# Delta-rule stage: the order on TensorE prices changes between plain and rounded matmuls and holds fill matmuls together in fours

## The chip, the cores and the metric

The kernel runs on one core of one Trainium2 chip. The metric is the device time of one execution in microseconds (us), the median over several runs. The core has TensorE (PE in the profile, with its weight loads as PEld), VectorE (DVE), ScalarE (ACT), GpSimd (POOL) and DMA queues issued from SyncE (SP).

## The reference

One layer of a hybrid backbone over 1024 latent tokens of width 1024, with 256 context tokens in front. The parts that matter here:

- `h = rms_norm(x) * (1 + scale) + shift`, then one input projection `h @ w_in` into many column groups: q, k, v of branch A, its gate z, q, k, v and gate of branch B, and merge gates.
- Branch A, the gated delta rule, in chunks of 128 tokens here (8 heads, two directions, 2 context chunks and 8 latent chunks each). Per chunk the state goes on as
  `v_new = u - w @ S`, `S' = S * exp(g_last) + k_dec^T @ v_new`, and the output is `q_dec @ S + qk @ v_new`. The triangular inverse behind `u` and `w` is made ahead of this, once for each head.
- Branch B, differential softmax attention (8 heads, two score maps each).
- Both branches are gated, projected, merged and sent through the output projection.

All results are float32.

## The kernel before, in words

The program is one long order of instructions per engine, written by a planner in Python when the kernel is built. Every piece of work is a generator ("stream") that yields steps of the form (engine, planned duration, what it depends on, how to issue it). The planner keeps a clock for each engine, asks each stream for its next step, chooses one, issues it and moves that engine's clock on. What it decides is only the order in which instructions stand on the engines; the chip then runs each engine's list in that order, and waits at semaphores where data is not there. There are two choosers. `flow` (line 75) takes, of all streams, the step with the smallest planned start plus bias. `turn_flow` (line 100) picks among steps that could start first on the same engine, within 0.02 us, by a priority; for the attention these come from the table `ABIAS` (line 1746), to which `due` (line 1438) adds 1.0 per tile of scores.

The stages in order of time are: the front (modulation, norm, transposes) and the convolution of q, k, v, both by `turn_flow`; the delta rule with everything that runs beside it, by `flow` (line 786); the attention and the merge of branch A, again by `turn_flow`; the output of branch B and the last projection.

In the stage that `flow` orders, TensorE has two kinds of work:

- **Fill.** The projections that nothing here waits for. Each operand is held as a rounded high part and a rounded low part (type fp32r), and a product is three rounded matmuls (high by high, high by low, low by high). `part_flow` (line 929) makes q, k, v of branch B in ten parts with outputs 256 wide, and then `fill_flow` (line 905) makes 32 gate units of 128 columns, each unit two halves of 24 matmuls 512 wide. In the profile their tile is `mm`. The fill stream has no bias (`None`): it takes part in the choice with its planned start plus `FB0`, and so stands back by 0.05 us for any other step. `FB1` would take over from `FT` = 38 finished units on, but there are only 32.
- **Plain float32 matmuls** of the delta rule. `scan` (line 1289) is the recurrence, one stream for each direction. A chunk is three dependent matmuls with a VectorE or ScalarE step between each two: `chain<-S,sk`, then `r` on VectorE, `chain<-r,x`, then `vd` on ScalarE, `chain<-vd,kk`, then `S` on VectorE. `out_chunk` adds two matmuls `out`. A plain matmul of 128 columns is two rows in the profile. `gdn_prep` (line 1082) prepares a head: `gram` matmuls in five groups, a substitution of 31 steps on VectorE, then four bursts of small matmuls (`pz`, `p`, `pz`, `pu`), and a store. Two preps are under way at a time: that of head h starts when head h-2 is stored, and `gram`, the substitution and the bursts each go head by head. The scan of a head needs the stored prep of that head and the scan of the head before.

For a step that needs a VectorE or ScalarE result, the planner reckons with a hand-over of 0.26 or 0.27 us plus `PEL` = 0.35 us before a matmul may be planned (table `LATENCY`, line 40).

`weights` and `part_weights` load and split the fill's weights into high and low parts on ACT, DVE and POOL; their bias is `WB` (line 1480). `flow` ends when the last head's tail (`tails`, line 1362: norm, gate, transposes `oT`) is planned and at least 32 - `LEFT` = 29 gate units are done. The rest of the gate units run in the next stage while the attention starts: its scores (`s`), softmax, transposes (`t`) and values (`v`) need memory that the delta rule gives free. In the attention, `sums`, `outs`, `lows` and `scales` are the queues of sums of squares, of squares of the outputs, of the low parts of transposed weights, and of the scaling of the second score map on ACT or POOL.

Of the kernel before, what the change touches and what calls it, by code (L numbers as in the profile page):

```python
# [34 lines left out]
PE, DVE, ACT, POOL, DMA, ADMA, DV2, PL1 = range(8)  # L35
# [8 lines left out]
class Block:  # L44
# [30 lines left out]
    def flow(self, until):  # L75


        clk = self.clk
        while not until():
            best = None  # L80
            for s in self.streams:
                self.ask(s)
            for s in self.streams:
                self.ask(s)
                h = s[2]
                if h is None or callable(h):
                    continue
                if s[3] is None:
                    s[3] = self.ready_at(h[0], h[2])
                start = self.begin_at(h[0], s[3])  # L90
                if s[1] is None:
                    start += self.FB0 if self.units_done < self.FT else self.FB1
                if h[0] == PE and len(h) > 4 and self.heat - self.HEAT * (start - clk[PE]) < 0:
                    start += self.COLD
                if best is None or start + (s[1] or 0.0) < best[0]:
                    best = (start + (s[1] or 0.0), s)
            assert best, "no stream can go on"
            self.step(best[1])

    def turn_flow(self, until):  # L100
# [613 lines left out]
    def run(self):  # L714
# [4 lines left out]
        with ExitStack() as left:  # L719
            self.hp, self.hs = self.spool(left, "hp"), {}  # L720
            self.hgroup(0)
            with ExitStack() as lw, ExitStack() as cx:
# [21 lines left out]
                with tc.manual_schedule(engines={E.PE, E.DVE, E.Activation, E.Pool, E.SP}):  # L744
# [25 lines left out]
                    def more():  # L770
                        yield lambda: sum(self.posted) == sum((NL if k == "q" else NT) // 2 for k, _ in parts)
                        cx.close()
                        self.gdn_more(gr)
                        yield lambda: False
                    for g, b in ((self.scan(0), "scan"), (self.scan(1), "scan"), (self.forever(self.outq[0]), "outq"),
# [4 lines left out]
                        self.stream(g, self.BIAS[b]) if g is not first else self.streams.append([g, self.BIAS[b], head, None])  # L780
                    self.stream(self.part_weights(parts), self.WB)
                    self.stream(self.weights(todo), self.WB)
                    self.stream(more())
                    self.stream(fill(), None)
                    self.MW = 2.5
                    self.flow(lambda: self.tailed == H and self.units_done >= len(todo) - self.LEFT)
                    gr.close()
# [645 lines left out]
    def named(self, n, gen):  # L1433
        s = self.entry[n] = [gen, self.ABIAS.get(n, 0), None, None]
        s[2] = next(gen, None)
        self.streams.append(s)

    def due(self, n, i):

        self.entry[n][1] = self.ABIAS.get(n, 0) + self.DUE * i  # L1440

# [35 lines left out]
    SPI = 0.5  # L1477
    MW = 0.0
    LAND = 2.5
    WB = -0.17  # L1480
    FT = 38
    LEFT = 3
    FB0 = 0.05
    FB1 = 0.36
    COLD = 0.4
    HEAT = 0.55
    HMAX = 0.55
# [244 lines left out]
    def side_start(self):  # L1732
# [10 lines left out]
    ONACT = (1, 2, 3)  # L1743
    TOL = 0.02
    PACE = 4.48
    ABIAS = dict(rels=-0.59, softs=8.84, norms=5.82, gateq=-27.29, sums=-18.71,
                 outs=-21.73, lows=-2.4, highs=-9.33, adds=36.19, scales=31.0, evs=22.29, mouts=-3.31,
                 att_out=1.9, turns=3.19, scores=-21.22, merge=25.46)
    KEEP = 3

# [454 lines left out]
```

## Time and profile before

| what | us |
|---|---|
| median of 3 runs (lowest to highest) | 1943.65 (1940.72 to 1945.57) |
| the profiled execution, its own time | 1943.38 |
| its span, first to last instruction | 1941.5 |
| PE busy in the span | 1901.2 |
| DVE busy | 1451.9 |
| ACT busy | 1065.9 |
| POOL busy | 679.2 |

A row of the profile is an instruction or a group of equal ones: start, length, engine, line, what it writes and reads, shape and count. All matmuls have the same line, that of a helper, and are told apart by their tiles. The ends of matmul rows are modelled and rows overlap, so what a matmul costs is read from start to start, not from the length of its row.

### The profile page before, as it was taken

How to read it: one execution, taken by the hardware profiler on the slowest of the kernel's cores; microseconds unless marked ns; L12 is line 12 of the kernel's file. 1: busy time of each engine (PE TensorE's matmuls, PEld its weight loads, DVE VectorE, ACT ScalarE, POOL GpSimd, SP SyncE). 2: the span in 40 equal slices, each digit the busy share in tenths (PEclk: the TensorE clock that was granted, in tenths of full speed). 3: DMA queues.
4: the chain of work that ended last, by engine and by line, in shares of the span. 5: the costliest groups of instructions: out<-in, count | busy, mean ns of one | idle time of the engine just before them, and what ended most of it. 6: DMA issues, size and time to landing. Idle time of an engine off the chain costs nothing.

```text
span 1941.5 us, 37467 instructions
## 1 busy us (share of the span) xinstructions
PE 1901.2 (98%) x13807; PEld 1675.8 (86%) x13807; DVE 1451.9 (75%) x3613; ACT 1065.9 (55%) x2191; POOL 679.2 (35%) x610
## 2 busy tenths in 40 slices
PE   6999999999999999999999999999999999999999
PEld 4888888899999998888888878887898888888887
DVE  4687998948886888767864965337896979985577
ACT  4543444426233563677575645448885868883222
POOL 3200000005541332343433232325766657671203
PEclk9999999999999999999999999999999999999999
DMA  9144535575546557667686565665436474226542
GB/s 333 61 133 99 138 95 132 130 197 174 171 134 190 167 187 230 231 197 241 197 284 206 186 189 164 215 237 185 143 114 207 160 241 152 82 88 218 187 148 87
DMA packets 383038, 336.39 MB, mean 173 GB/s; under 512 B 142609, under 2 KB 323443, under 8 KB 381831
## 3 DMA queue, kind: packets, MB, share of 16 engines
q1 hardware_dynamic: 382855, 333.99, 54.6%
q8 instruction: 109, 1.79, 0.4%
q14 instruction: 74, 0.61, 0.1%
HBM read 222.14 MB, written 111.79 MB: 172 GB/s over the span
## 4 chain that ended last, share of the span: by engine, by line
PE 83%; DVE 6%; DMA 4%; ACT 3%; issue 2%; SPq 1%; POOL 1%; DVEq 0%; ACTq 0%; POOLq 0%
PE mm L56 42%; PE s L56 6%; PE v L56 5%; PE chain L56 5%; PE mb L56 5%; PE ma L56 4%; PE x L56 3%; PE t L63 3%; PE out L56 3%; DVE S L1562 1%; PE gram L56 1%; DVE ac L595 1%; PE tr L63 1%; PE pz L56 1%; PE mp L56 1%
## 5 line engine op out<-in xcount | busy, mean ns | idle before, releaser
L56 PE MATMUL mm<-hs,wh 128*128 128x512 f32 (+1 forms) x2048 | 648.3, 390 | 1.5 <-DVE hs L408 1.4
L56 PEld LDWEIGHTS mm<-hs,wh 128*128 128x128 f32 x2048 | 371.1, 189 | 58.6 <-DVE hs L408 1.9
L56 PE MATMUL mm<-hs,wl 128*128 128x512 f32 (+1 forms) x1024 | 397.4, 388 | 1.0 <-POOL wl L885 1.0
L56 PE MATMUL mm<-wh,hs 128*128 128x256 f32 (+1 forms) x1792 | 332.7, 286 | 0.2 <-ACT sq L977 0.2
L56 PEld LDWEIGHTS mm<-wh,hs 128*128 128x128 f32 x1792 | 280.8, 191 | 0.7 <-ACT sq L977 0.4
L1562 DVE TENSOR_SCALAR_CACHE_REDUCE S<-s,rsq 128x512 f32<-128x512 f32 (+1 forms) x384 | 239.0, 654 | 27.6 <-PE s L56 14.2
L56 PE MATMUL mm<-wl,hs 128*128 128x256 f32 (+1 forms) x896 | 255.6, 285 | 0.0
L1599 POOL TENSOR_TENSOR S<-S 128x1280 f32<-128x1280 f32 x64 | 188.6, 2951 | 90.6 <-ACT S L1592 88.5
L56 PEld LDWEIGHTS mm<-hs,wl 128*128 128x128 f32 x1024 | 193.8, 189 | 29.8 <-POOL wl L885 1.4
L1575 ACT ACTIVATE S<-S,mn 128x1280 f32<-128x1280 f32 x128 | 175.2, 1371 | 53.2 <-DVE mn L1574 53.1
L56 PEld LDWEIGHTS mm<-wl,hs 128*128 128x128 f32 x896 | 171.3, 191 | 0.1
L595 DVE SCALAR_TENSOR_TENSOR ac<-xc,convT,ac 128x1284 f32<-128x1284 f32 (+1 forms) x96 | 138.8, 1448 | 11.5 <-ACT ac L593 10.8
L56 PE MATMUL s<-kk,qh 128*128 128x512 f32 (+1 forms) x384 | 143.6, 374 | 2.3 <-DVE S L1562 1.7
L56 PE MATMUL s<-kk,ql 128*128 128x512 f32 (+1 forms) x384 | 133.8, 360 | 0.0
L1636 DVE TENSOR_TENSOR al<-t,ah 128x512 fp32r<-128x512 f32 (+1 forms) x192 | 106.8, 595 | 7.6 <-ACT ah L1631 6.2
L580 POOL MEMSET xc<- 128x2 f32 (+1 forms) x64 | 3.6, 99 | 298.2 <-ACT sq L629 113.2
L1157 DVE TENSOR_TENSOR ts<-ts,tmp 80x31 f32<-80x31 f32 (+15 forms) x248 | 93.8, 378 | 6.0
L1155 DVE TENSOR_TENSOR tmp<-ab,ts 80x31 f32<-80x31 f32 (+15 forms) x248 | 91.4, 368 | 6.1 <-DMA ab<-da 0.7
L56 PE MATMUL ma<-y,wh 128*128 128x512 f32 x256 | 93.3, 410 | 1.9 <-DVE g L1808 1.9
L1320 ACT ACTIVATE vd<-chain,edk 128x128 f32<-128x128 f32 x144 | 52.2, 370 | 75.8 <-PE chain L56 70.4
L1631 ACT CAST ah<-t 128x512 fp32r<-128x512 f32 (+1 forms) x192 | 87.8, 520 | 9.3 <-PE t L63 8.9
L56 PE MATMUL v<-al,vh 128*128 128x256 f32 x320 | 90.7, 284 | 0.4 <-DVE al L1636 0.3
(296 smaller groups left out, 4317.1 us busy)
## 6 DMA issues: line engine op xcount, KB each, us to landing
wr<-in_w_in_dram SPq DMA_DIRECT2D x48, 512.0 KB, 5.7
hx<-in_w_in_dram SPq DMA_DIRECT2D x64, 256.0 KB, 4.2
x<-xq SPq DMA_DIRECT2D x64, 256.0 KB, 5.0
X<-gcd SPq DMA_DIRECT2D x8, 1280.0 KB, 8.8
kd<-col SPq DMA_DIRECT2D x40, 256.0 KB, 2.2
xq<-X SPq DMA_DIRECT2D x16, 640.0 KB, 8.8
kk<-kd SPq DMA_DIRECT2D x16, 640.0 KB, 5.8
kq<-gkq SPq DMA_DIRECT2D x8, 1152.0 KB
```

Source lines behind the costliest of these rows:

```text
L56: self.nc.tensor.matmul(out, lhsT, rhs, start=start, stop=stop)
L63: self.nc.tensor.transpose(out, src, self.ident[:src.shape[0], :src.shape[0]])
L580: x["e"].append((yield PL1, 0.1, [old], lambda: nc.gpsimd.memset(xc[:, a:b], 0.0)))
L595: t = yield DV2, 1.21e-3 * wd, [t], lambda: nc.vector.scalar_tensor_tensor(ac[:, :wd], xc[:, j:j + wd], self.convw(j, x["ct"]), ac[:, :wd] ...
L1155: t = yield DV2, n * w / 960.0 + 0.08, [t if j else self.later(t, 2.5), t1], lambda: V.tensor_tensor(tv, ab[:, j + 1:, j:j + 1].to_broadca ...
L1157: t = yield DV2, n * w / 960.0 + 0.08, [t, t1], lambda: V.tensor_tensor(ts[:, j + 1:, :w], ts[:, j + 1:, :w], tv, ALU.subtract)
L1320: td = yield ACT, 0.251, [t], lambda: nc.scalar.activation(vd, pc[:, 1], AF.Copy, scale=self.edk[:, c, g:g + 1])
L1562: e = yield DVE, 0.675 if m == 512 else 0.408, [e, self.sfree[c].get(n - 4 + c)], lambda: self.nc.vector.tensor_scalar(x["S"][c][:, o:o + ...
L1575: x["x"].append((yield ACT, 1.36, [e], lambda: nc.scalar.activation(S, S, AF.Exp, bias=x["mn"][:, c:c + 1], scale=-1.0, accum_out=w["l0"][ ...
L1599: e = yield POOL, 2.9, [e], lambda: self.nc.gpsimd.tensor_tensor(S0, S0, S1, ALU.add)
L1631: e = yield ACT, 0.48 if nb == 4 else 0.27, [t, y["old", k]], lambda: self.nc.scalar.copy(y["ah", k][:, :, q], pv)
L1636: t = yield DVE, 0.603 if k < 2 else 0.322, [e, y["old", k]], lambda: self.nc.vector.tensor_tensor(y["al", k][:, :, q], pv, y["ah", k][:, ...
```

## The change

In `flow` only, four things are new.

1. `SWITCH`: a fill step that follows a step of another stream on TensorE gets 0.086 us added to its planned duration.
2. `SWF`: right after such another step, the fill stands back by a further 0.2 us, 0.25 us with `FB0`.
3. `RUN`, `SWC`: after one, two or three fill matmuls in a row, a step of any other stream on TensorE stands back by 0.62 us. From the fourth on it doesn't.
4. `streak` counts this: the number of fill matmuls in a row, or -1 after another step.

Then weights are different: `WB` goes from -0.17 to -0.38 (the weight streams take part in the choice 0.21 us earlier), `FB1` from 0.36 to 0.46, and in the attention's table `sums` and `outs` come later (by 2.82 and 7.78), `lows` and `scales` sooner (by 2.11 and 3.7). No instruction is added or removed; what moves is the order on the engines and the DMA queue.

```diff
@@ flow
                 if s[1] is None:
                     start += self.FB0 if self.units_done < self.FT else self.FB1
+                    start += self.SWF if self.streak < 0 else 0.0
+                elif h[0] == PE and 0 < self.streak < self.RUN:
+                    start += self.SWC
...
             assert best, "no stream can go on"
+            if best[1][2][0] == PE:
+                fill = best[1][1] is None
+                if fill and self.streak < 0:
+                    h = best[1][2]
+                    best[1][2] = (h[0], h[1] + self.SWITCH) + tuple(h[2:])
+                self.streak = max(self.streak, 0) + 1 if fill else -1
             self.step(best[1])
@@ class Block
-    WB = -0.17
+    WB = -0.38
     FT = 38
     LEFT = 3
+    SWITCH, RUN, streak = 0.086, 4, 0
+    SWF = 0.2
+    SWC = 0.62
     FB0 = 0.05
-    FB1 = 0.36
+    FB1 = 0.46
...
-    ABIAS = dict(rels=-0.59, softs=8.84, norms=5.82, gateq=-27.29, sums=-18.71,
-                 outs=-21.73, lows=-2.4, highs=-9.33, adds=36.19, scales=31.0, evs=22.29, mouts=-3.31,
+    ABIAS = dict(rels=-0.59, softs=8.84, norms=5.82, gateq=-27.29, sums=-15.89,
+                 outs=-13.95, lows=-4.51, highs=-9.33, adds=36.19, scales=27.3, evs=22.29, mouts=-3.31,
                  att_out=1.9, turns=3.19, scores=-21.22, merge=25.46)
```

## The prediction

> **What bounds the kernel now.** I read the page's totals and its chain first, then the busy time in stretches cut at the stage borders, then what TensorE waited for, and last the order of matmuls inside the delta rule.
>
> ```profile
> PE 83%; DVE 6%; DMA 4%; ACT 3%; issue 2%; SPq 1%; POOL 1%; DVEq 0%; ACTq 0%; POOLq 0%
> ```
>
> ```profile
> 752.00:1269.00 517.00, 513.32 (x4588) 448.57 (x4587) 341.18 (x1006) 317.22 (x930) 180.10 (x238) 1.00 0.68 215
> ...
> 1320.00:1330.00 10.00, 5.94 (x31) 4.33 (x30) 4.88 (x17) 9.47 (x13) 4.16 (x2) 1.00 0.44 147
> 1330.00:1340.00 10.00, 10.00 (x65) 9.27 (x64) 7.24 (x25) 6.62 (x12) 4.85 (x2) 0.83 1.03 379
> 1340.00:1720.00 380.00, 375.54 (x2444) 331.84 (x2442) 326.27 (x1106) 299.74 (x506) 255.22 (x128) 1.00 0.46 154
> ```
>
> The columns of a stretch are its length, busy time of PE, PEld, DVE, ACT and POOL with instruction counts, granted clock, DMA share and GB/s. TensorE carries 83% of the chain and is covered by rows nearly everywhere: 513.3 of 517 us while the scans run. The one visible hole is at the start of the attention, 4.1 us in 1320 to 1330, and right after it the granted clock is 0.83 for 10 us. Covered is not the same as efficient, so I ask next whether TensorE waits, and whether a change of matmul kind costs time. What it waited for between 440 and 1300:
>
> ```profile
> PE p L56 <- DVE Z L1177: 1.4, 1, 1.4
> PE tr L63 <- DVE fin L999: 1.3, 1, 1.3
> PE mm L56 <- POOL wl L885: 1.0, 1, 1.0
> ```
>
> The rest of that list is shorter still. TensorE hardly waits, so this stage can become cheaper only if its matmuls do.
>
> **Part 1, the price of a change of kind.** The timeline of TensorE, two kinds mixed, then plain alone, then fill alone:
>
> ```profile
> 821.60 0.39 PE L56 MATMUL mm<-hs,wh 128*128 128x512 f32 x1
> 821.83 0.38 PE L56 MATMUL chain<-S,sk 128*128 128x128 f32 x2
> 821.97 0.48 PE L56 MATMUL mm<-hs,wh 128*128 128x512 f32 x1
> 822.28 0.38 PE L56 MATMUL chain<-S,sk 128*128 128x128 f32 x2
> ...
> 825.48 0.39 PE L56 MATMUL chain<-vd,kk 128*128 128x128 f32 x2
> 825.71 0.39 PE L56 MATMUL out<-vn,x 128*128 128x128 f32 x2
> 825.93 0.39 PE L56 MATMUL chain<-vd,kk 128*128 128x128 f32 x2
> 826.15 0.39 PE L56 MATMUL out<-vn,x 128*128 128x128 f32 x2
> ...
> 1274.66 0.39 PE L56 MATMUL mm<-hs,wl 128*128 128x512 f32 x1
> 1274.89 0.62 PE L56 MATMUL mm<-hs,wh 128*128 128x512 f32 x2
> 1275.34 0.39 PE L56 MATMUL mm<-hs,wl 128*128 128x512 f32 x1
> ```
>
> Three fills alone take 1275.34 - 1274.66 = 0.68, 0.227 each. Three plain matmuls (two rows each) take 826.15 - 825.48 = 0.67, 0.223 each. The first fill after a plain matmul has a row of 0.48 instead of 0.39 us, which is where a price of 0.086 can be read. But that row also begins early: 0.14 us after the plain matmul's first row, where the next plain one begins 0.22 after. Start to start, 821.60 to 822.28 is 0.68 us and holds two fills and one plain matmul, 2 x 0.227 + 0.223 = 0.677. The change and its return cost 0.003. A whole chunk of both scans, with the rows of fill, of `chain` and of `out`:
>
> ```profile
> 821.83:826.85 5.02, 4.15 (x13) 2.05 (x12) 0.00 (x0) 0.00 (x0) 1.00 0.27 79
> 821.83:826.85 5.02, 2.30 (x13) 2.12 (x12) 1.40 (x4) 1.06 (x4) 1.00 0.27 79
> 821.83:826.85 5.02, 1.54 (x8) 1.36 (x8) 0.42 (x2) 0.10 (x1) 1.00 0.27 79
> ```
>
> Less one row each that overlaps an edge, these are 12 fills and 20 rows of plain, ten matmuls: 12 x 0.227 + 10 x 0.223 = 4.95 of 5.02 us. The fills stand there in six runs, so a change costs at most 0.07 / 6 = 0.011 us. At 0.086 the chunk would take 5.47.
>
> [...]
>
> How many changes go? I count 344 runs of fill in the timeline from the first to the last of these rows:
>
> ```profile
> 752.42 0.40 PE L56 MATMUL mm<-hs,wl 128*128 128x512 f32 x1
> 1268.28 0.39 PE L56 MATMUL mm<-hs,wl 128*128 128x512 f32 x1
> ```
>
> 114 are of one matmul, 94 of two, 50 of three. Those 258 hold 452 fills, 113 runs of four, so about 145 changes go. At 0.011: **-1.6 us** (0 to -12.5).
>
> **Part 2, what the plain matmuls lose.** To bring the short runs to four takes 114 x 3 + 94 x 2 + 50 = 580 fills, 1.7 for each of the 344 runs, 0.38 us. By so much a plain matmul that heads a group stands later than today. That is no work, only order; it costs where the scan's end decides. The scans' last three borders, and the last bursts of the prep of the seventh head (index 6):
>
> ```profile
> 1116.60 0.38 PE L56 MATMUL out<-vn,x 128*128 128x128 f32 x2
> 1137.40 1.22 PE p L56 x76
> 1151.09 1.31 PE pu L56 x40
> 1173.33 0.38 PE L56 MATMUL chain<-vv,x 128*128 128x128 f32 x2
> 1227.33 0.60 PE L56 MATMUL chain<-vv,x 128*128 128x128 f32 x4
> 1268.73 0.39 PE L56 MATMUL out<-vn,x 128*128 128x128 f32 x2
> ```
>
> No scan runs from 1116.6 to 1173.3: head 6 waits for its prep. From there two scans of ten chunks, 95.4 us, lead to the end. So the end is prep of head 6, then 20 chunks. A delay of any earlier scan is free, and in that pause the fill runs are long, so the bursts lose nothing.
>
> For the 20 chunks, the fill in their stretch, and after it:
>
> ```profile
> 1173.00:1269.00 96.00, 71.04 (x220) 37.00 (x219) 0.00 (x0) 5.39 (x9) 1.00 0.59 187
> 1269.00:1320.00 51.00, 43.45 (x177) 32.22 (x178) 0.00 (x0) 4.19 (x7) 1.00 0.54 186
> ```
>
> That is 11 fills per chunk. In the new order both scans' steps are ready together after each run of four (0.91 us against a planned hand-over of about 1.07), which makes three runs, 12 fills per chunk: +1 x 20 x 0.227 = 4.5. By the code, the four bursts of the last head's prep and two groups of transposes of head 6 also stand between 1173 and the end: six more heads of groups at 0.38, 2.3, of which I count 2. Together **+6.5 us**; from below 0 (the scans are as dense as in the chunk shown, which has its 12 already), from above 3 x 20 x 0.38 = 23 (every step of the chain waits by itself). I take the low end's side because the chunk shown is the nearest row.
>
> For the prep, five `gram` groups of head 6 and nine groups of head 4, which must be stored before prep 6 may start, can fall while scans run: 14 x 0.38 = 5.3 at most, 0 at least, or a gain if VectorE is freer for the substitution. Much of a prep is VectorE and DMA, so I take **+3 us**.
>
> Does later order mean later end? After the scan 177 fills are left, and they cover the tail and the start of the attention. Each microsecond by which the scan ends later has been spent on fill that is then missing here. The hole in 1320 to 1330 shows that this cover is used up already, so the delay counts in full.
>
> [...]
>
> **Part 3, the stand-back of 0.25 us.** After a plain matmul the planner may now leave TensorE idle in its plan for up to 0.25 us for another plain one. On the chip the operand is there earlier:
>
> ```profile
> 1267.57 0.35 DVE L1311 SCALAR_TENSOR_TENSOR r<-chain,eg,vv 128x128 f32<-128x128 f32 x1 [0.17 <-PE chain L56]
> 1268.52 0.38 PE L56 MATMUL chain<-r,x 128*128 128x128 f32 x2
> ```
>
> `r` ends at 1267.92 and its reader starts 0.60 later. That reserve hides a planned 0.25, and also the 0.075 by which the plan overrates a change. **0 us**; were the reserve gone, half of 0.25 at perhaps one in four of the 199 runs left, 6 us.
>
> **Part 4, weights.** `FB1` is never read. `WB` puts weight loads and splits earlier; TensorE waited 1.0 us for a split (`wl` above), so 0, between -1.0 and, as the splits take ACT and DVE from the scan, +1.0. The four attention weights shift order between 1300 and 1720, where TensorE waited for:
>
> ```profile
> PE t L63 <- DVE al L1636: 2.1, 1, 2.1
> PE t L63 <- ACT zo L1036: 1.7, 1, 1.7
> PE s L56 <- DVE S L1562: 1.2, 4, 0.4
> PE m L63 <- DVE g L1808: 0.8, 1, 0.8
> ```
>
> The rest of that list is as short or shorter. At best these 5.8 us go; DVE is busy 86% of 1340 to 1720, so an order as much worse is as near. I take **0**.
>
> **Sum.** -1.6 + 6.5 + 3 + 0 + 0 = +7.9 on the profiled execution's own 1943.4 (0.3 under the median shown): 1951.3, said as **1951**.
>
> **The rivals.** *Slower as forecast*, 0.44. With each chain step waiting (+23) and the preps whole (+5.3) it reaches 1970.
>
> *No change*, 0.30. The scans fall into step and keep 12 fills per chunk, as the chunk at 821.83 has; the preps hide behind VectorE. Then -1.6 stands alone with some scatter: 1942. For it: that chunk is already 5.02 us for exactly what the rule wants. Against: 11 per chunk where it counts.
>
> *Faster, by the attention*, 0.18. The new weights take out the waits of 1300 to 1720: -5.8 - 1.6 gives 1936. It decides if these waits shrink by more than the scan's end moves; `outs` and `sums` going behind `lows` favours the 2.1 us on `al`. Against: one wait each, so a new order can make new ones.
>
> *Faster, because the long row is real*, 0.08. If fill after plain costs 0.086 in a way that the starts do not show, 145 x 0.086 = 12.5: 1931. The chunk's sum speaks against it.
>
> **How the numbers follow.** About 0.3% (5.8 us) is what a measurement of this kernel can tell from no change: 1937.8 to 1949.5. Faster is 0.18 + 0.08 = 0.26, same 0.30, slower 0.44. The range reaches down to 1935, just past the attention rival's figure, leaving out the last rival and the far side of that one, and up to 1966, short of the upper bound of 1970 with all waits paid: about 2 in 10 lie outside. The likeliest case alone is 1949 to 1970.
>
> **What the new profile would show.** Right: runs of fill of four in the delta rule, about 200 instead of 344; fill start to start unchanged at 0.227 and a plain matmul at 0.223; head 6 starting after 1173 and the last `out` some 10 us after 1268.7; fewer than 177 fills after it and a hole larger than 4.1 us at the attention's start. Wrong: a chunk with 12 fills that takes clearly under 4.95 us (then a change had a price); the last `out` before 1265; TensorE waits for `r`, `S` or `vd` of more than a few microseconds in sum (then the reserve was too small); a gain that all lies after 1340.

## The result, and the profile after

The changed kernel takes 1947.43 us, the median of 19 runs (1944.19 to 1950.89), against 1943.09 for the kernel before in as many runs (1940.72 to 1946.98). The ratio is 1.0022, with a 95% interval of 1.0015 to 1.0029: 4.3 us longer. That lies inside the 0.3% which the prediction called no change, and inside its range, about half as far up as the 1951 that it named. Most of its terms, though, were something else on the chip, as the rest of this document shows.

The profiled execution of the changed kernel took 1950.19 us, 2.8 above its median, and that of before 1943.38. So 6.8 us of span are to be found in the traces, of which about 4 are the change. The totals of the changed kernel's chain:

```profile
PE 55%; DVE 4%; ACT 3%; DMA 2%; issue 1%; SPq 0%; POOL 0%; DVEq 0%; ACTq 0%
```

The chain's shares come to 65% here, where those of before come to 100. The page doesn't say where the missing third went, so I place nothing by the chain. What follows goes by stretches. The columns are, as before, the length, busy time of PE, PEld, DVE, ACT and POOL, the granted clock, the DMA share and GB/s. The changed kernel:

```profile
427.00:470.00 43.00, 40.17 (x324) 39.76 (x323) 21.78 (x52) 27.83 (x67) 14.94 (x10) 0.96 0.58 197
...
759.00:1273.00 514.00, 510.57 (x4563) 446.26 (x4562) 347.64 (x1019) 313.70 (x927) 180.08 (x238) 1.00 0.68 215
1298.00:1320.00 22.00, 19.26 (x90) 15.17 (x88) 17.54 (x56) 15.38 (x20) 9.44 (x4) 1.00 0.74 250
1320.00:1330.00 10.00, 10.00 (x46) 8.29 (x45) 2.42 (x12) 9.08 (x11) 2.95 (x1) 1.00 0.14 55
1330.00:1340.00 10.00, 8.36 (x47) 6.69 (x45) 2.94 (x6) 5.15 (x9) 2.94 (x1) 0.99 0.42 131
```

Before, the stretches 427 to 470 and 1298 to 1320:

```profile
427.00:470.00 43.00, 42.60 (x355) 41.88 (x354) 25.64 (x62) 31.45 (x73) 18.54 (x12) 1.00 0.66 229
1298.00:1320.00 22.00, 22.00 (x105) 18.07 (x104) 17.12 (x63) 17.05 (x21) 7.23 (x4) 1.00 0.64 228
```

Three things are to be seen. In 427 to 470 the changed kernel gets 324 matmuls done where before does 355. While the scans run TensorE is as covered as ever (510.6 of 514). And the hole at the start of the attention has moved but not shrunk: before it is 4.1 us of 1320 to 1330, with nothing in the stretches on either side; now there is nothing in 1320 to 1330, but 2.7 in 1298 to 1320 and 1.6 in 1330 to 1340, 4.4 in all.

Rows that cover TensorE do not say whether its matmuls are late, so I subtracted from the time of each stretch what its matmuls need at their usual distance from start to start (0.227 us for a fill of 512 columns, 0.1115 for a row of a plain one, and so on, all from the trace of before). What is left over is "lost" below. Lost more than before, by stage of the changed kernel's profiled execution:

| stage | lost more than before, us |
|---|---|
| up to 427, where nothing was changed | +1.9 |
| 427 to 470 | +3.8 |
| 470 to 752 | +1.6 |
| the scans, 752 to 1272 | +2.0 |
| from there to 1770, the scans' tail and the attention | -4.1 |
| 1770 to the end | +1.4 |

The sum is 6.6 of the 6.8. The +1.9 stands ahead of the change, in an unchanged part, and belongs to this one execution; the other lines give 4.7, near the 4.3 of the medians. The -4.1 does not lie at the start of the attention. From the last matmul of the scans (`out`) to the 145th row of the scores (`s`, at 1377.5 before and 1387.2 after), 10.2 us are lost after and 8.7 before. The gain comes behind that row: from there to the end 16.4 are lost after and 20.5 before.

**The order did what the rule says.** The timeline of TensorE in the last scan, changed kernel:

```profile
1229.75 0.39 PE L56 MATMUL chain<-S,sk 128*128 128x128 f32 x2
1229.90 0.47 PE L56 MATMUL mm<-hs,wl 128*128 128x512 f32 x1
1230.21 0.62 PE L56 MATMUL mm<-hs,wh 128*128 128x512 f32 x2
1230.66 0.40 PE L56 MATMUL mm<-hs,wl 128*128 128x512 f32 x1
1230.90 0.39 PE L56 MATMUL mm<-hs,wh 128*128 128x512 f32 x1
1231.13 0.38 PE L56 MATMUL chain<-r,x 128*128 128x128 f32 x2
```

Fill now stands in runs of four or a little more, with the plain matmuls of both directions grouped between them. Counted over the scans there are 215 runs where there were 344, and 174 of them hold exactly four.

**The end of the scans.** Fill matmuls in the last scan of ten chunks, and after the scans, changed kernel:

```profile
1225.50:1272.90 47.40, 34.74 (x120) 20.47 (x121) 0.00 (x0) 3.00 (x5) 1.00 0.57 189
...
1273.00:1334.00 61.00, 50.53 (x209) 38.16 (x207) 0.00 (x0) 4.78 (x8) 1.00 0.48 164
```

The last scan before:

```profile
1227.30:1270.60 43.30, 33.29 (x98) 16.52 (x98) 0.00 (x0) 2.39 (x4) 1.00 0.71 240
```

Both stretches go from the first matmul of the scan to the last `out`. The last scan is 4.1 us longer and holds 120 fills instead of 98, 12 per chunk instead of 9.8. 22 x 0.227 = 5.0: all of its extra length is fill. And after the scan there are 209 fills left, not fewer than before but 31 more (178 before by the same count; the prediction's window had 177).

### The profile page after: what moved, and what is told of

Read it like the earlier page. It is cut to its first block, busy times and chain, and to the rows that moved or that the text cites. A ratio compares the mean times of both kernels' runs of the same rounds, so it can differ in the third digit from the quotient of the medians.

```text
span 1948.3 us, 37458 instructions
## 1 busy us (share of the span) xinstructions
PE 1905.8 (98%) x13807; PEld 1680.1 (86%) x13807; DVE 1452.0 (75%) x3613; ACT 1061.6 (54%) x2189; POOL 677.9 (35%) x610
## 4 chain that ended last, share of the span: by engine, by line
PE 55%; DVE 4%; ACT 3%; DMA 2%; issue 1%; SPq 0%; POOL 0%; DVEq 0%; ACTq 0%
PE mm L56 17%; PE s L56 7%; PE v L56 6%; PE mb L56 5%; PE chain L56 5%; PE ma L56 4%; PE x L56 3%; PE t L63 3%; PE out L56 2%; PE gram L56 1%; DVE S L1574 1%; PE pz L56 1%; PE z L56 1%; ACT X L1113 0%; DVE al L1648 0%
## 5 line engine op out<-in xcount | busy, mean ns | idle before, releaser
L56 PE MATMUL mm<-hs,wh 128*128 128x512 f32 (+1 forms) x2048 | 635.6, 387 | 1.5 <-DVE hs L417 1.4
L604 DVE SCALAR_TENSOR_TENSOR ac<-xc,convT,ac 128x1284 f32<-128x1284 f32 (+1 forms) x96 | 138.5, 1447 | 10.7 <-ACT ac L602 10.1
L63 PE MATMUL t<-ct,S 128*128 128x128 f32 x640 | 89.6, 273 | 2.8 <-DVE al L1648 2.8
## 6 DMA issues: line engine op xcount, KB each, us to landing
X<-gcd SPq DMA_DIRECT2D x8, 1280.0 KB, 10.6
kq<-gkq SPq DMA_DIRECT2D x8, 1152.0 KB, 10.1
```

Of the source, the lines that this page charges most:

```text
L56: self.nc.tensor.matmul(out, lhsT, rhs, start=start, stop=stop)
L63: self.nc.tensor.transpose(out, src, self.ident[:src.shape[0], :src.shape[0]])
L604: t = yield DV2, 1.21e-3 * wd, [t], lambda: nc.vector.scalar_tensor_tensor(ac[:, :wd], xc[:, j:j + wd], self.convw(j, x["ct"]), ac[:, :wd] ...
```

## The experiments

All times are against the kernel before, run on the same chip in the same job (its median was 1942.4, 1944.21 and 1944.01 in the three jobs). Lines marked - and + are against the kernel before, unless the diff says that it is against the kernel after.

### What a change of kind costs

```diff
-    B = Block(ctx, tc, a)
-    B.out = out
-    B.run()
+    for n, g in (("wa", 96), ("fa", 1), ("fb", 2), ("fc", 4), ("fd", 12), ("fe", 96)):
...
+        for r in range(96 // g):
+            for i in range(r * g, r * g + g):
+                nc.tensor.matmul(f, wr[:, i % 8], xr, start=i == 0, stop=i == 95)
+            for i in range(r * g, r * g + g):
+                nc.tensor.matmul(p[:, 0:P], w[:, i % 8], x[:, 512:512 + P], start=True, stop=True)
```

This kernel leaves out all of the block's computation. Each stretch has 96 rounded matmuls of 512 columns and 96 plain ones of 128, in alternating runs of 1, 2, 4, 12 and 96.

> The kernel's work is left out whole; only matmuls of its two kinds run, with nothing to wait for: 96 rounded ones of 512 columns and 96 plain ones of 128 columns in each of five stretches, in turn one by one (fa, pa), two by two (fb, pb), four by four (fc, pc), twelve by twelve (fd, pd), and 96 by 96 (fe, pe). If a change of kind costs at most 0.011 us, as the starts in the kernel before say, a stretch takes 96 x 0.227 + 96 x 0.223 = 43.2 us and the one by one stretch at most 95 x 0.011 = 1.0 us more than the 96 by 96 one. If it costs 0.086, as the row's length says, one by one takes 95 x 0.086 = 8.2 us more, two by two 4.0, four by four 2.0.

Measured, the rounded matmuls of each stretch (row length in ns as least, median, most; then first and last start in us):

```profile
L2180 PE MATMUL fa<-xr,wr x96: 476/477/481, 51.8 to 94.9; 128*128 128x512 f32 x96
...
L2180 PE MATMUL fb<-xr,wr x96: 387/434/478, 95.3 to 137.9; 128*128 128x512 f32 x96
...
L2180 PE MATMUL fc<-xr,wr x96: 387/393/479, 138.5 to 181.0; 128*128 128x512 f32 x96
...
L2180 PE MATMUL fd<-xr,wr x96: 389/389/476, 182.1 to 222.5; 128*128 128x512 f32 x96
...
L2180 PE MATMUL fe<-xr,wr x96: 389/389/476, 225.4 to 247.0; 128*128 128x512 f32 x96
```

From one stretch's first start to the next one's, one by one takes 43.5 us, in twos 43.2, in fours 43.5, in twelves 43.3. The last stretch, 96 and then 96, takes 43.3 from its first start to the end of its last plain pass. 95 changes more or less move the sum by at most 0.3 us, 0.003 each. In the same rows the median row length falls from 477 to 389 ns. So the 0.086 is how the record of a fill after a plain matmul is drawn, and no time of TensorE. There was nothing for the rule to save.

### The parts alone

The rule alone, with the old `WB` and the old attention weights, is the change without these lines of it:

```diff
against the kernel after
-    WB = -0.38
+    WB = -0.17
...
-    ABIAS = dict(rels=-0.59, softs=8.84, norms=5.82, gateq=-27.29, sums=-15.89,
-                 outs=-13.95, lows=-4.51, highs=-9.33, adds=36.19, scales=27.3, evs=22.29, mouts=-3.31,
+    ABIAS = dict(rels=-0.59, softs=8.84, norms=5.82, gateq=-27.29, sums=-18.71,
+                 outs=-21.73, lows=-2.4, highs=-9.33, adds=36.19, scales=31.0, evs=22.29, mouts=-3.31,
```

> The rule in flow (SWITCH, SWF, SWC, RUN) with the old WB and the old attention weights. Theory 1, the rule itself costs TensorE time (waits where plain or transposing steps were held back, among them 2.8 us and a clock dip in the first 40 us of the stage): 1946 to 1950, with waits of over 2 us between 427 and 475 again. Theory 2, the rule is neutral and the new weights cost: 1941 to 1944.5. Theory 3, a change really costs 0.086, the rule gains some 12 us and the weights lose more: below 1936.

Measured: 1956.41 us, ratio 1.0072 (1.0060 to 1.0084), +14. In its profiled execution the scans end at 1293.7, 23 later than before, with 144 fills left, and between 470 and the scans' end 14.8 us more are lost than before, 6 of them before the scans begin. What TensorE waited for in that kernel while the scans ran:

```profile
PE chain L56 <- ACT vd L1329: 2.4, 3, 1.5
PE p L56 <- issue: 1.6, 3, 0.6
PE chain L56 <- DVE S L1342: 1.2, 3, 0.6
PE chain L56 <- DMA x<-xq: 1.0, 1, 1.0
...
PE chain L56 <- DVE r L1320: 0.6, 2, 0.4
```

These lines are 6.8 us together. Other losses are in pieces too small for this view; Part 3 below counts those between plain matmuls.

```diff
-    WB = -0.17
+    WB = -0.38
```

> The kernel before with WB at -0.38 alone. Theory 1 (the rule costs): 1942 to 1945, no wait of over 1 us between 427 and 475. Theory 2 (the weights cost): 1945 to 1950, and the waits of the first 40 us of the stage are here. Theory 3: above 1950.

Measured: 1949.91 us, ratio 1.0040 (1.0028 to 1.0052), +7.5. Its profiled execution is 4.4 us over that of before, of which 3.7 are lost between 427 and 470. TensorE's waits from 427 to 475 in this kernel, in the kernel after, and in the kernel before:

```profile
PE mm L56 <- ACT sq L977: 2.1, 1, 2.1
PE tr L63 <- DVE col L1018: 0.8, 1, 0.8
```

```profile
PE mm L56 <- ACT sq L986: 1.8, 1, 1.8
PE tr L63 <- DVE col L1027: 1.0, 1, 1.0
```

```profile
PE mm L56 <- ACT sq L977: 0.2, 1, 0.2
```

The same two waits as in the kernel after, at the same place. Before, the first is 0.2 us and the second isn't listed. The orders on POOL and ACT show where they come from. The rows are the split of a weight (`wl`), the finishing of a part's result (`fin`), the cast of its transpose (`col`) and the emptying of PSUM (`raw`), first before, then after. Everything here stands 2.0 us later in the changed kernel from the start.

```profile
443.59 1.23 POOL L1007 TENSOR_TENSOR fin<-fin,ss 128x512 f32<-128x512 f32 x1
444.79 2.58 POOL L885 TENSOR_TENSOR wl<-wr,wh 128x1024 fp32r<-128x1024 f32 x1
...
446.95 0.58 ACT L1017 CAST col<-tr 128x512 fp32r<-128x512 f32 x1
...
451.40 0.63 ACT L976 COPY raw<-mm 128x256 f32<-128x256 f32 x2
```

```profile
445.59 2.40 POOL L894 TENSOR_TENSOR wl<-wr,wh 128x1024 fp32r<-128x1024 f32 x1
447.94 2.03 POOL L1016 TENSOR_TENSOR fin<-fin,ss 128x512 f32<-128x512 f32 x1
...
452.17 0.56 ACT L1026 CAST col<-tr 128x512 fp32r<-128x512 f32 x1
...
456.76 0.62 ACT L985 COPY raw<-mm 128x256 f32<-128x256 f32 x2
```

Before, `fin` goes first. After, the split stands in its place and `fin` behind it. The first `col` then comes 3.2 us later than the 2.0 would have it, and the next emptying of PSUM 3.4. By the code, these steps (`evacs`, `posts`) have a bias of -0.3: a `WB` of -0.17 stands behind it, one of -0.38 ahead of it, so that preparing later fill goes before the steps that the present fill needs. On POOL `wl` is ahead of this `fin` in all six orders with a `WB` of -0.38 or -0.39, the four of the sections below among them, and behind it in all seven others.

```diff
-    ABIAS = dict(rels=-0.59, softs=8.84, norms=5.82, gateq=-27.29, sums=-18.71,
-                 outs=-21.73, lows=-2.4, highs=-9.33, adds=36.19, scales=31.0, evs=22.29, mouts=-3.31,
+    ABIAS = dict(rels=-0.59, softs=8.84, norms=5.82, gateq=-27.29, sums=-15.89,
+                 outs=-13.95, lows=-4.51, highs=-9.33, adds=36.19, scales=27.3, evs=22.29, mouts=-3.31,
```

> The kernel before with the four new attention weights alone. The order up to 1282 is that of the kernel before. Theory 1 (the rule costs, and the attention gave 4 us of it back): 1938 to 1941. Theory 2 (the weights cost): above 1944.5. If what the attention gave back came from the 31 more fills left for its start and not from its weights: 1942 to 1945.

Measured: 1941.95 us, ratio 0.9991 (0.9980 to 1.0001). The total shows no clear change, but a place does. From the 145th row of the scores to the last instruction, in one execution each, the five orders of this document with the old attention weights take 562.9 to 564.5 us and the eight with the new ones 560.8 to 561.8, with work that differs by at most ten matmuls of the merge. Before takes 564.0, the new weights alone 561.8, the kernel after 561.1. So the new weights do shorten the attention and what follows it, by 2 to 3 us; which of the four does it, no run shows.

The parts do not add up: +14, +7.5 and -0.5 make 21, and together they take 4.3. That raised the question of what any new order costs, whatever its idea.

### Steps that mean nothing

Two changes far too small to have a purpose, which only make the planner choose differently here and there:

```diff
-    WB = -0.17
+    WB = -0.18
```

> The kernel before with WB at -0.18 instead of -0.17: a step of 0.01 us that has no meaning of its own, but lets the planner choose otherwise at some places. Theory 1 (the weight streams overtake the emptying of PSUM banks because their bias passes that of the evacuation, -0.3): within 3 us of before, no wait of TensorE over 1 us for sq near 457. Theory 2 (any other order of this stage moves the time by several us, and the order of before is a good draw): 2 to 10 us slower, with waits at places that no bias explains.

Measured: 1952.52 us, ratio 1.0047 (1.0035 to 1.0060), +8.3. -0.18 does not pass the -0.3 of the emptying, and the two waits of 427 to 470 aren't there (1.4 us lost, before 1.1).

```diff
-    FB0 = 0.05
+    FB0 = 0.051
```

> The kernel before with FB0 at 0.051 instead of 0.05. Theory 1: within 2 us of before. Theory 2 (scatter by order): another time than before by 2 us or more, of either sign, with the excess of TensorE over its own work in the delta rule moved by as much.

Measured: 1951.51 us, ratio 1.0044 (1.0031 to 1.0058), +7.3. TensorE's longest waits from 427 to 1300:

```profile
PE p L56 <- issue: 5.9, 3, 3.5
PE oT L63 <- POOL oa L1389: 3.6, 1, 3.6
```

They stand at steps on which no bias was moved. A thousandth of a microsecond in one planned start costs 7 us. Beside these two neighbours the kernel before is a good draw, and a difference of this size between two orders says nothing by itself about the rule that made them. From here on I went by places in the trace more than by totals.

### The rule without the stand-back, and without the false price

```diff
against the kernel after
-    SWF = 0.2
+    SWF = 0.0
```

> The kernel after with SWF at 0: fill no longer stands back 0.2 us after a plain matmul. Theory 1 (the stand-back makes TensorE wait inside groups of plain matmuls, since the reserve of 0.35 us does not hide it): the time lost from one plain matmul to the next in the scans, 3.3 us before and 7.7 after, falls back to about 3.5. Theory 2 (it is scatter): it stays at 6 to 10. The total says less, as the order moves everywhere: 1943 to 1958.

```diff
against the kernel after
-    SWITCH, RUN, streak = 0.086, 4, 0
+    SWITCH, RUN, streak = 0.0, 4, 0
```

> The kernel after with SWITCH at 0: the plan no longer holds each fill after a plain matmul to be 0.086 us longer. Theory 1 (the false price makes the plan run behind TensorE, which then arrives early and waits): the time lost from one plain matmul to the next falls from 7.7 to 4 to 6 us. Theory 2 (the price is harmless, the stand-back alone or scatter makes the waits): 7 us or more. Total 1940 to 1955.

Measured: 1955.16 us, 1.0064 (1.0050 to 1.0079), without the stand-back, and 1950.72 us, 1.0037 (1.0022 to 1.0051), without the price. From one plain row to the next one the scans lose 4.6 and 4.0 us, where the kernel after loses 7.7. So this loss shrinks when either is taken away. Without the stand-back, though, another grows: from a fill to a plain matmul behind it 8.6 us are lost, where the kernel after loses 2.7. In all, the bursts of small matmuls left out, the scans lose 12.8 us before, 15.2 after, 17.6 without the stand-back and 11.2 without the price. With the bursts, where the kernel without the price waits once for 3.4 us, it is 2.0, 5.8 and 1.7 more than before. Both kernels are longer than the kernel after also because their scans end later (at 1304.8 and 1297.4) and use up more fill: 74 and 73 are left. Then, without the price, at the start of the attention:

```profile
PE s L56 <- DMA ql<-qd: 7.2, 1, 7.2
```

This is a hole at the stage where before has its 4.1 us, though it ends with a load here and before with ACT and DVE. Too little fill stands in front of it: the last one starts 7.8 us before the wait ends. Without the stand-back the same wait is 5.2 us.

### Neighbours of both kernels

Four more orders, to see how far the draw goes on each side. Two with the rule, each with a weight moved by 0.01:

```diff
against the kernel after
-    WB = -0.38
+    WB = -0.39
```

> The kernel after with WB at -0.39 instead of -0.38, a step without a meaning of its own. If small steps off the kernel before cost 8 to 9 us because that order is a good draw, the kernel after, whose weights were chosen too, should behave alike: 1950 to 1960. If the rule makes the order less touchy (fewer choices are close): within 2 us of the kernel after, 1945.5 to 1949.5. The time lost between plain matmuls stays above 6 us either way, as SWF and SWITCH are both there.

```diff
against the kernel after
-    SWF = 0.2
+    SWF = 0.21
```

> The kernel after with SWF at 0.21 instead of 0.2. As for the step of WB: 1950 to 1960 if the order is a draw, 1945.5 to 1949.5 if the rule steadies it. Time lost between plain matmuls above 6 us.

Two without runs of four and with the price cut to 0.004, about what the first experiment left of it:

```diff
against the kernel after
-    WB = -0.38
+    WB = -0.17
-    SWITCH, RUN, streak = 0.086, 4, 0
-    SWF = 0.2
+    SWITCH, RUN, streak = 0.004, 0, 0
+    SWF = 0.0
-    FB0 = 0.05
+    FB0 = 0.04
-    BIAS = dict(scan=0, outq=0, evacs=-0.3, posts=-0.3, preps=0, tails=0, sets=-0.3, loads=-0.5, asides=0)
+    BIAS = dict(scan=0, outq=0.02, evacs=-0.3, posts=-0.3, preps=0, tails=0, sets=-0.3, loads=-0.5, asides=0)
```

> No rule (RUN 0, SWF 0, a price of 0.004 us for a change, WB as before), the new attention weights, FB0 at 0.04 and the bias of the output chunks at 0.02: another draw, with short runs of fill allowed. If runs of four were worth anything, it is slower than the kernel after. If they are not, and scatter rules: between 1938 and 1953, time lost between plain matmuls 2.5 to 5.5.

```diff
against the kernel after
-    WB = -0.38
+    WB = -0.3
-    SWITCH, RUN, streak = 0.086, 4, 0
-    SWF = 0.2
+    SWITCH, RUN, streak = 0.004, 0, 0
+    SWF = 0.05
```

> No runs (RUN 0), a stand-back of 0.05 instead of 0.2 us, a price of 0.004 for a change, WB at -0.30, just level with the evacuations' bias, the new attention weights. Scatter: between 1938 and 1953; time lost between plain matmuls 3 to 6, less than with a stand-back of 0.2. If a WB at or beyond the evacuations' -0.3 alone makes fill wait for sq near 457, that wait of 2 us is here.

Measured, with the others of their kind:

| order | us | ratio (95%) | fills left after the scans | lost in the 130 us after them |
|---|---|---|---|---|
| before | 1942.40 to 1944.21 | 1 | 178 | 10.1 |
| `WB` -0.38 alone | 1949.91 | 1.0040 (1.0028 to 1.0052) | 133 | 8.7 |
| `WB` -0.18 | 1952.52 | 1.0047 (1.0035 to 1.0060) | 136 | 10.6 |
| `FB0` 0.051 | 1951.51 | 1.0044 (1.0031 to 1.0058) | 211 | 7.9 |
| no rule, `FB0` 0.04, `outq` 0.02 | 1943.96 | 1.0004 (0.9993 to 1.0014) | 249 | 6.0 |
| no rule, `WB` -0.30 | 1941.28 | 0.9981 (0.9971 to 0.9990) | 192 | 8.9 |
| after | 1947.43 | 1.0022 (1.0015 to 1.0029) | 209 | 9.8 |
| rule alone | 1956.41 | 1.0072 (1.0060 to 1.0084) | 144 | 9.7 |
| after, `SWF` 0 | 1955.16 | 1.0064 (1.0050 to 1.0079) | 74 | 15.9 |
| after, `SWITCH` 0 | 1950.72 | 1.0037 (1.0022 to 1.0051) | 73 | 18.3 |
| after, `WB` -0.39 | 1945.14 | 1.0004 (0.9996 to 1.0013) | 240 | 6.3 |
| after, `SWF` 0.21 | 1949.72 | 1.0036 (1.0025 to 1.0048) | 181 | 7.1 |

Without the rule the orders other than before reach from 0.9981 to 1.0047, with it from 1.0004 to 1.0072. The two groups overlap, and five or six draws don't separate them. Neither neighbour of the kernel after came out as expected: 1945.14 lies just below the range for a steadier order, 1949.72 between the two ranges. The last column shows what the fill left over is worth: from 249 down to 133 the loss after the scans moves between 6 and 11 us, and at 74 and 73 it is 16 and 18.

The order without runs and with `WB` at -0.30 beats both kernels, by 0.19% (0.10 to 0.29) against before. The stretch 427 to 470 in it:

```profile
427.00:470.00 43.00, 42.34 (x353) 41.77 (x352) 27.26 (x70) 31.19 (x72) 19.37 (x12) 1.00 0.69 240
```

353 matmuls, 355 before: -0.30 does not pass the emptying of PSUM. Behind the 145th row of the scores this order loses 15.6 us where before loses 20.5, so most of its gain lies in the attention, with the new weights; for the rest I claim no place.

## Why the prediction came out near, and where its steps failed

The total was near because errors of both signs met. Step by step:

**Part 1, the price of a change: right.** It was taken as at most 0.011 us against the planner's 0.086, and measured as at most 0.003. 129 runs of fill went where 145 were forecast. The term of -1.6 becomes -0.4 or less, and the rival by which the long row is real has fallen.

**Part 2, later scans: the count per chunk was right, the path to the end and "the delay counts in full" were wrong.** It forecast 12 fills per chunk in the last chunks, which is what the last scan now holds, and that scan is 4.1 us longer. But its last `out` comes only 2.2 us later, at 1272.7 instead of 1270.5 (behind the row at 1268.73, which the prediction took for the last one, two more follow). And the scans as a whole, from the first `chain` to the last `out`, take 513.5 us instead of 517.8; their end is later only because they begin 6.6 later. The step that failed first is "the end is prep of head 6, then 20 chunks". Head 6, forecast to start after 1173, starts at 1149.9:

```profile
1149.92 0.38 PE L56 MATMUL chain<-vv,x 128*128 128x128 f32 x2
```

Its prep was not 3 us later, as the +3 had it, but 22 sooner: its last `pu` stands at 1130 instead of 1152. Now the last scan is the one that waits for its prep: between the two scans no plain matmul of theirs runs for 27 us, where before it was 7. The last `pu` of that prep stands at 1203.3, before at 1197.0. So the end became the prep of head 7, then ten chunks. In all 13 traces of the whole kernel the last `out` follows the last `pu` by 63 to 84 us. The rule alone, whose scans end 23 us later, has its last `pu` 24 us later.

The other step that failed is the one from the end of the scans to the end of the kernel. Of the 177 fills after the scan the prediction said that the hole "shows that this cover is used up already, so the delay counts in full". Fill done inside the scan is fill not done elsewhere, and fill moved from one place to the other costs little while enough is left over (in the orders above 6.0 to 10.6 us are lost behind the scans with 133 to 249 fills left, 15.9 and 18.3 with 74 and 73). Over the whole stage the changed order holds less fill, not more: 209 are left, so "fewer than 177 fills" was wrong. "A hole larger than 4.1 us" came true by 0.3, but in two pieces, and the first of them stands while fill is still left (the last fill starts at 1333.9). By the orders above cover runs out between 133 and 74. The 4.1 us that come back behind the scans come with the attention weights, not with the fill.

**Part 3, "0 us": wrong, +4.4.** The reserve was read from one operand that was there 0.60 us early. In the changed kernel it is gone in more places. One case from the timelines of TensorE, its weight loads and VectorE, around 903:

```profile
903.16 0.39 PE L56 MATMUL out<-vn,x 128*128 128x128 f32 x2
903.55 0.59 DVE L1342 SCALAR_TENSOR_TENSOR S<-S,egl,chain 128x128 f32<-128x128 f32 x2
903.94 0.56 PEld L56 LDWEIGHTS chain<-S,sk 128*128 128x128 f32 x4 [0.58 <-DVE S L1342]
903.94 0.75 PE L56 MATMUL chain<-S,sk 128*128 128x128 f32 x4 [0.40 <-DVE S L1342]
```

The next plain matmul starts 0.78 us after `out`, not 0.22, as it waits for `S`. Its weight load is not ahead of it but begins with it, and then its first row takes 0.21 to the next instead of 0.11. Counted are the places in the scans, behind a plain matmul, that lose more than 0.03 us. From one plain tile to another there are 10 in the changed kernel with 3.0 us in sum, and 3 with 0.9 before. From a row to the next of the same tile there are 36 with 2.6, and 6 with 0.4 before; most of these are 0.1 or less, below what the list of waits shows. All that is lost from one plain row to the next, summed over the scans, is 3.3 us before, 7.7 after and 10.6 with the rule alone. The neighbours without the rule have 3.0 to 5.3. With both the stand-back and the price in the plan it is 6.9 to 12.1, without one of them 4.0 and 4.6. So this loss comes with the pair. That the plan takes plain matmuls nearer to their operands fits the places counted, but is not shown by itself, and why it takes both, the runs don't show. The prediction's own bound, 6 us if the reserve is gone, was the right size. The sign it named to look for, TensorE waiting for `r`, `S` or `vd` for more than a few microseconds, would have missed it, as the list of waits in the kernel after shows:

```profile
PE chain L56 <- DVE S L1342: 1.0, 2, 0.6
PE chain L56 <- DMA sk<-gkq: 0.5, 1, 0.5
...
PE chain L56 <- DVE r L1320: 0.2, 1, 0.2
```

Over the whole scan stage about half of it is offset by smaller losses elsewhere (15.2 against 12.8, the bursts left out).

**Part 4, `WB` "0, between -1.0 and +1.0": wrong.** All six orders with -0.38 or -0.39 lose 2.7 to 3.8 us more than before between 427 and 470, and all those with -0.17, -0.18 or -0.30 at most 0.4 more. The prediction looked at what the weight streams feed and take from the scan, not at the steps of the present fill that the new bias overtakes. The attention weights, taken as 0, are worth 2 to 3 us in the attention itself, and the time lost there falls by 4.1. That is less than the -5.8 of the rival, which had the place and the sign right; its total of 1936 was wrong, as the other terms outweigh the gain.

**The rivals.** By the bound of 0.3% the result is "no change", but not as that rival had it: it let nothing move and came to 1942, 5 us short, while here 3.8 (`WB`), 1.6 and 2.0 are lost and 4.1 come back in the attention. "Slower as forecast" has the right sign and 12 fills per chunk, not the rest of its mechanism.

What stays open: whether runs of four, with no false price and no stand-back, help or hurt by themselves. No order here separates that from the scatter of 7 us that a meaningless step brings. Where the +8.3 and +7.3 of the two smallest steps arise was followed only in part.

## What to carry to other kernels

Read a matmul's price from start to start before you build a planning rule on it: in the first experiment the stretch with rows of 477 ns took 43.5 us and the last one, with rows of 389, 43.3. When a bias of a stream is moved, list the biases of all streams that share its engine and see which ones it overtakes. And where an order is made by a greedy planner, run a step that means nothing first: here it moved the time by 0.4%, more than the change under study, so a single total proves nothing about a rule, and only a place that all variants with the edit share does, as the one near 450 does for `WB` and the attention for its weights.

## What was not expected of the hardware

Behind two short waits of TensorE, of 1.03 and 1.80 us, the granted clock was 0.50 for 3.41 us. The timeline of TensorE around 459 in the kernel after (what ended a wait, and its length, in brackets):

```profile
453.60 0.63 PE L63 MATMUL tr<-ct,fin 128*128 128x128 f32 x4 [1.03 <-DVE col L1027]
...
457.93 0.39 PE L56 MATMUL mm<-wh,hs 128*128 128x256 f32 x1 [1.80 <-ACT sq L986]
```

and the stretch behind it, with its granted clock, below another stretch at half clock:

```profile
141.81:145.22 3.41, 3.35 (x10) 2.58 (x11) 3.41 (x4) 1.39 (x4) 0.00 (x0) 0.50 0.00 0
459.25:462.66 3.41, 3.41 (x19) 3.41 (x18) 3.31 (x9) 2.56 (x6) 2.70 (x3) 0.50 0.00 0
```

Waits of 1.03 and 1.80 us, 4 us apart and with matmuls between them, were followed by 3.41 us at a clock of 0.50, in which 1.5 are lost. It isn't decided by the length of the waits alone. With `WB` at -0.39 the same two waits, of 1.0 and 1.8 us, leave the clock at 1.00:

```profile
427.00:470.00 43.00, 39.88 (x330) 39.07 (x330) 24.54 (x60) 28.90 (x68) 16.39 (x11) 1.00 0.62 214
```

The stretches at half clock that hold matmuls start at 141.81, 459.25 and 1339.89 in the kernel after. 317.44 / 93 and 880.64 / 258, their distances over whole numbers, are both 3.413, and such a stretch is 3.41 long. In windows of this length counted from these starts, the wait of 1.80 lies whole in the one that ends at 459.25; the wait of 1.03 lies in the window ahead of that, and behind it the clock is 1.00. The windows just ahead of the other two stretches have 2.03 and 1.64 us without a matmul row, and the one ahead of the half clock at 1331.10 in the kernel before has 2.12. Time without rows does not decide it alone either: in the kernel after, the window from 664.05 to 667.46 has 1.87, and the clock behind it is 1.00:

```profile
664.05:667.46 3.41, 1.54 (x14) 1.54 (x15) 2.36 (x6) 0.80 (x2) 0.55 (x1) 1.00 0.25 82
667.46:670.87 3.41, 3.41 (x32) 3.41 (x31) 3.38 (x7) 1.78 (x5) 0.00 (x0) 1.00 0.70 242
```

What decides between 1.64 and 1.87, the traces don't show.
